# The second weight tile of each in-projection unit split by ScalarE and an accumulating DMA instead of VectorE

## The chip, the core and the metric

The kernel runs on one core of a Trainium2 chip. The metric is the device time of one execution in microseconds, taken as the median of several runs. The engines are TensorE (PE), which multiplies matrices; VectorE (DVE) and ScalarE (ACT), which work on tiles in the on-chip memories; GpSimd (POOL), a slower general engine; and SyncE (SP), which here only issues DMAs. Each engine takes its instructions in one fixed order and waits where the next one's data is not there. A DMA issued by POOL stands in POOL's order like any other instruction.

## What is computed

Two layers of a recurrent decoder run over a prompt of 512 positions and 8 sample sequences of 8, 576 columns in all. The part of a layer that matters here, cut from the reference:

```python
proj = (h @ lw['w_in']).astype(f32)
(hg_q, hg_f, hg_i, hg_g, gla_q, gla_k, gla_v, gla_a, gla_g, rw_cols,
 ret_q, ret_k, ret_v, ret_g, gate_logits) = _split(proj, IN_WIDTHS)
# four recurrent mixers (HGRN2, GLA, RWKV-7, RetNet) on their columns
up = jnp.einsum('blnc,ncd->blnd', branches, lw['w_branch'])
merged = jnp.sum(gates * up, axis=2).astype(h.dtype)
y = merged @ lw['w_out']
# then x + y, and x + SwiGLU(RMSNorm(x))
```

`h` is the normalised input with 1024 features; all weights are float32.

## The kernel before

All large products are made in float16 with both operands split in two: a float32 weight w becomes `hi`, the float16 of WS·w, and `lo`, the float16 of WS·w − hi. For each 128 by 128 block PE runs three matmuls, hi·hi (L241), hi·lo of the input (L242) and lo·hi (L243), in `gemm`. Only L243 reads the weight's `lo`.

The input projection is cut into units of 128 output columns, 46 in each layer. `w_in` calls `wload` for one: 1024 rows are 8 blocks of 128, so a unit has two tiles of 128 by 512, g = 0 with blocks 0 to 3 and g = 1 with blocks 4 to 7 (PE goes through blocks 0 to 3 first). SP loads a tile into one of four `raw` buffers (float32); ACT writes `hi` (L228), DVE writes `lo` (L229), both into a `whl` tile of a ring of four ("w"; the first two units of a layer use a ring "rd"). `wload` is also called for the branch, output and feed-forward weights.

The units of a layer follow a fixed list in `mix_units`: six HGRN units first, then RWKV, GLA, the rest of HGRN, and the RetNet units with the gate columns between and behind them. `mix` advances them in turn with generators that run the recurrences of the units before, so that PE has projection work while DVE and ACT work on the recurrences. The order of instructions on each engine comes out of a scheduler that walks this program; a reader sees it in the order rows further down. In the HGRN stage ACT computes tanh and a scaled copy of a projection (L498 `th`, L499 `pcp`, written as a gated product by DVE in L500), loads function tables, and evacuates `hg_v` (L487); POOL computes `gd` (L980, L981) from `hg_q` and `hg_k`. In the start of a layer ACT squares the input (L306), takes the norm's root (L319, L320), and casts the normalised input to `h` (L464), which PE waits for. In the gate units ACT evacuates the projection (L1458) and the mixed tokens (L248 `bo` and `mt`). POOL's L901 is a large product in the RWKV part, and L1709 an accumulating DMA in the feed-forward part, from one float32 buffer onto another.

Of the kernel before, what the change touches and what calls it, by code (L numbers as in the profile page):

```python
# [13 lines left out]
AF = mybir.ActivationFunctionType  # L14
ALU = mybir.AluOpType
PSUM = bass.MemoryType.PSUM
ADD, SUB, MUL, MAX, MIN = ALU.add, ALU.subtract, ALU.mult, ALU.max, ALU.min
# [8 lines left out]
KT = D // 128  # L26
WS = 256.0
# [147 lines left out]
class Net:  # L175
# [29 lines left out]
        return self.pc[:, c:c + 1]  # L205


    def wload(self, pieces, nk, ncols, rings=("w",)):


        nc = self.nc
        step = GW // ncols
        tiles, parts = [], []
        for g, k0 in enumerate(range(0, nk, step)):
            kn = min(step, nk - k0)
            n = kn * ncols
            raw = self.wp.tile([128, GW], F32, tag="raw", name="raw")
            rv = raw[:, :n].rearrange("p (k c) -> p k c", k=kn)
            for ap, off, w in pieces:
                nc.sync.dma_start(out=rv[:, :, off:off + w],  # L220
                                  in_=ap[128 * k0:128 * (k0 + kn)].rearrange("(k p) c -> p k c", p=128))
            if not parts:
                ring, rings = rings[0], rings[1:] or rings
                c = SIZE[ring] // (4 * GW)
                hl = self.t(ring, [128, c, 2, GW], "whl", F16)
                parts = [hl[:, i] for i in range(c)]
            hl = parts.pop(0)
            nc.scalar.activation(hl[:, 0, :n], raw[:, :n], AF.Copy, scale=WS)  # L228
            nc.vector.scalar_tensor_tensor(hl[:, 1, :n], raw[:, :n], WS, hl[:, 0, :n], op0=MUL, op1=SUB)  # L229
            tiles.append(hl[:, :, :n].rearrange("p a (k c) -> p a k c", k=kn))  # L230
        return lambda k: (tiles[k // step][:, 0, k % step], tiles[k // step][:, 1, k % step])

# [245 lines left out]
            yield  # L478

    def w_in(self, l, pieces, n):  # L480
        return self.wload([(self.io["w_in"][l][:, c:c + w], o, w) for c, o, w in pieces], KT, n, self.rings_in)

    def copy_evac(self, dst, scale):
        nc = self.nc
# [1469 lines left out]
```

## Time and profile before

| | us |
|---|---|
| median of 3 runs | 2200.16 |
| lowest, highest | 2197.33, 2200.17 |
| the profiled execution | 2207.72 |
| its span | 2205.9 |
| PE busy | 2039.1 |
| DVE busy | 1636.6 |
| ACT busy | 1081.3 |
| POOL busy | 682.3 |
| in-projection and mixing, layer 0 and layer 1 | 0 to 510, 1100 to 1600 |

Durations further down are of the profiled execution, which took 7.6 us more than the median. The busy times overlap; the chain of waits, followed back from the last instruction, tells which piece of work ended last at each time. A row of a timeline gives start, duration, engine, line, operation and tiles, and in square brackets the idle time before it with what ended it.

### The profile page before, as it was taken

The numbers are of one execution on the slowest core, as the hardware profiler recorded it, in microseconds if no ns is written. First come the engines' busy times: TensorE is split into PE (matmuls) and PEld (weight loads), VectorE is DVE, ScalarE is ACT, GpSimd is POOL, SyncE is SP. The second block draws the span as 40 slices with busy tenths as digits, with TensorE's granted clock in tenths as the row PEclk, the third lists the DMA queues.
The fourth block names the chain that finished last, engine by engine and source line by source line (L and its number), as shares of the span: only waits on it lengthen the run. The fifth ranks groups of instructions, "written<-read, shape, count | busy, mean of one in ns | idle before, by whom it ended". The sixth has DMA issues, their size and how long they took to land.

```text
span 2205.9 us, 42236 instructions
## 1 busy us (share of the span) xinstructions
PE 2039.1 (92%) x15754; PEld 1612.3 (73%) x15754; DVE 1636.6 (74%) x3409; ACT 1081.3 (49%) x2524; POOL 682.3 (31%) x889
## 2 busy tenths in 40 slices
PE   7989999998888899999999889989998988999998
PEld 5767787786676677777777778768776766777776
DVE  7889667768785899863488986586788779998441
ACT  6554546345444555442466355453645465554332
POOL 2223222146550544320012142213465316443000
PEclk9999999999999999999999999999999999999999
DMA  6312224333435344343421222242343443443331
GB/s 181 84 41 62 58 58 110 77 83 92 116 98 177 80 116 120 87 135 103 122 68 46 58 62 60 73 111 62 87 120 88 131 141 97 111 116 87 121 106 51
DMA packets 373498, 209.59 MB, mean 95 GB/s; under 512 B 59810, under 2 KB 360410, under 8 KB 373292
## 3 DMA queue, kind: packets, MB, share of 16 engines
q1 hardware_dynamic: 365516, 192.73, 31.6%
q0 software_dynamic: 7776, 14.16, 3.6%
q8 instruction: 124, 2.03, 0.4%
q14 instruction: 82, 0.67, 0.1%
HBM read 173.72 MB, written 16.59 MB: 86 GB/s over the span
## 4 chain that ended last, share of the span: by engine, by line
PE 47%; DVE 28%; ACT 8%; issue 7%; DMA 5%; POOL 3%; SPq 1%; DVEq 0%; ACTq 0%; POOLq 0%
PE pb L243 5%; PE pb L242 5%; PE pb L241 5%; PE xb L243 4%; PE xb L242 4%; PE xb L241 4%; DVE hA L1704 4%; DVE hS L1704 3%; DVE sc L1745 2%; DVE fy L1776 2%; DVE whl L229 2%; DVE su L1745 2%; PE fsS L1731 2%; PE fsS L1729 2%; PE fsS L1730 2%
## 5 line engine op out<-in xcount | busy, mean ns | idle before, releaser
L241 PE MATMUL pb<-h,whl 128*128 128x288 f16 (+1 forms) x1504 | 435.8, 290 | 4.4 <-ACT h L464 2.2
L243 PE MATMUL pb<-h,whl 128*128 128x288 f16 (+1 forms) x1504 | 435.5, 290 | 3.2 <-DVE whl L229 3.1
L242 PE MATMUL pb<-h,whl 128*128 128x288 f16 (+1 forms) x1504 | 436.0, 290 | 0.6 <-DVE h L465 0.4
L229 DVE SCALAR_TENSOR_TENSOR whl<-raw,whl 128x512 f16<-128x512 f32 (+1 forms) x352 | 253.8, 730 | 134.3 <-ACT whl L228 132.2
L242 PEld LDWEIGHTS <-whl 128*128 128x128 f16 (+1 forms) x2784 | 275.4, 99 | 88.0 <-issue 13.5
L243 PEld LDWEIGHTS <-whl 128*128 128x128 f16 (+1 forms) x2784 | 275.1, 99 | 88.0 <-issue 12.7
L241 PEld LDWEIGHTS <-whl 128*128 128x128 f16 (+1 forms) x2784 | 277.2, 100 | 76.6 <-issue 3.6
L228 ACT ACTIVATE whl<-raw 128x512 f16<-128x512 f32 (+1 forms) x352 | 213.3, 618 | 168.2 <-PE pb L243 51.9
L243 PE MATMUL xb<-fa,whl 128*128 128x288 f16 x704 | 201.3, 286 | 0.0
L242 PE MATMUL xb<-fa,whl 128*128 128x288 f16 x704 | 201.3, 286 | 0.0
L241 PE MATMUL xb<-fa,whl 128*128 128x288 f16 x704 | 201.3, 286 | 0.0
L1729 PE MATMUL fsA<-h,hA 128*128 128x288 f16 x432 | 124.3, 288 | 14.9 <-DVE gu L1550 10.8
L1729 PE MATMUL fsS<-st,hS 128*128 128x288 f16 x456 | 132.6, 291 | 5.9 <-ACT hS L1703 5.9
L1731 PE MATMUL fsS<-st,hS 128*128 128x288 f16 x456 | 132.4, 290 | 0.4 <-DVE hS L1704 0.3
L1730 PE MATMUL fsS<-st,hS 128*128 128x288 f16 x456 | 132.5, 291 | 0.0
L1731 PE MATMUL fsA<-h,hA 128*128 128x288 f16 x432 | 124.2, 288 | 1.7 <-DVE hA L1704 1.6
L1730 PE MATMUL fsA<-h,hA 128*128 128x288 f16 x432 | 124.3, 288 | 0.0
L1707 POOL TENSOR_TENSOR raw<-raw 128x512 f32<-128x512 f32 x52 | 79.0, 1520 | 134.2 <-DVE hA L1704 129.7
L1729 PEld LDWEIGHTS <-hS 128*128 128x128 f16 x864 | 85.7, 99 | 35.9 <-ACT hS L1703 13.7
L1704 DVE SCALAR_TENSOR_TENSOR hA<-sraw,hA 128x512 f16<-128x512 f32 x110 | 103.1, 945 | 10.6 <-ACT hA L1703 10.6
L1707 POOL TENSOR_TENSOR sraw<-sraw 128x512 f32<-128x512 f32 x60 | 89.7, 1499 | 51.4 <-DVE hA L1704 45.7
L1731 PEld LDWEIGHTS <-hS 128*128 128x128 f16 x864 | 85.7, 99 | 24.8 <-DVE hS L1704 2.6
(486 smaller groups left out, 5257.8 us busy)
## 6 DMA issues: line engine op xcount, KB each, us to landing
raw<-in_w_in SPq DMA_DIRECT2D x208, 256.0 KB
sraw<-in_w_ffn_in SPq DMA_DIRECT2D x40, 512.0 KB
raw<-in_w_ffn_out SPq DMA_DIRECT2D x80, 256.0 KB
raw<-in_w_ffn_in SPq DMA_DIRECT2D x78, 256.0 KB
x<-xd SPq DMA_DIRECT2D x32, 288.0 KB
raw<-sraw POOLq DMA_DIRECT2D x34, 256.0 KB, 3.3
sraw<-in_w_in SPq DMA_DIRECT2D x32, 256.0 KB
raw<-in_w_out SPq DMA_DIRECT2D x32, 256.0 KB
```

The costliest lines, as they stand in the source:

```text
L228: nc.scalar.activation(hl[:, 0, :n], raw[:, :n], AF.Copy, scale=WS)
L229: nc.vector.scalar_tensor_tensor(hl[:, 1, :n], raw[:, :n], WS, hl[:, 0, :n], op0=MUL, op1=SUB)
L241: nc.tensor.matmul(ps, wh, hi, start=i == 0, stop=False)
L242: nc.tensor.matmul(ps, wh, lo, start=False, stop=False)
L243: nc.tensor.matmul(ps, wl, hi, start=False, stop=i == len(ks) - 1)
L1704: nc.vector.scalar_tensor_tensor(hl[:, 1], a, WS, hl[:, 0], op0=MUL, op1=SUB)
L1707: nc.gpsimd.tensor_tensor(dst, a, b, op=op)
L1729: nc.tensor.matmul(ps, w[a][:, 0, k], hi, start=k == 0, stop=False)
L1730: nc.tensor.matmul(ps, w[a][:, 0, k], lo, start=False, stop=False)
L1731: nc.tensor.matmul(ps, w[a][:, 1, k], hi, start=False, stop=k == 3)
L1745: nc.vector.tensor_tensor(o, a, p, op=ADD)
L1776: nc.vector.scalar_tensor_tensor(y, u, PH * AS, sg, op0=MUL, op1=MUL)
```

## The change

`wload` hands the split to a new function, `wsplit`. For in-projection tiles with g = 1, 92 in the kernel, `lo` and `hi` are made without DVE. ACT writes −w as float16 into `lo` (L212). POOL issues a DMA that adds `lo`, cast to float32, onto the raw tile in place, so the raw tile holds w minus its float16 rounding (L213). ACT makes `hi` as −WS·lo (L214), which does not need the DMA, and, when the DMA has landed, writes `lo` as WS times the raw tile (L215). All other tiles keep the old pair, which now has the lines 217 and 218. From there on a line of the kernel after is 11 higher than the same line before (L228 and L229 are the exception: they moved into `wsplit`).

```diff
@@ -205,7 +205,19 @@
         return self.pc[:, c:c + 1]
 
-    def wload(self, pieces, nk, ncols, rings=("w",)):
+    def wsplit(self, hi, lo, w, dma):
+
+        nc = self.nc
+        if dma:
+            nc.scalar.activation(lo, w, AF.Copy, scale=-1.0)
+            nc.gpsimd.dma_start(out=w, in_=lo, accum_op=ADD)
+            nc.scalar.activation(hi, lo, AF.Copy, scale=-WS)
+            nc.scalar.activation(lo, w, AF.Copy, scale=WS)
+        else:
+            nc.scalar.activation(hi, w, AF.Copy, scale=WS)
+            nc.vector.scalar_tensor_tensor(lo, w, WS, hi, op0=MUL, op1=SUB)
+
+    def wload(self, pieces, nk, ncols, rings=("w",), dma=False):
 
         nc = self.nc
@@ -225,8 +237,7 @@
                 hl = self.t(ring, [128, c, 2, GW], "whl", F16)
                 parts = [hl[:, i] for i in range(c)]
             hl = parts.pop(0)
-            nc.scalar.activation(hl[:, 0, :n], raw[:, :n], AF.Copy, scale=WS)
-            nc.vector.scalar_tensor_tensor(hl[:, 1, :n], raw[:, :n], WS, hl[:, 0, :n], op0=MUL, op1=SUB)
+            self.wsplit(hl[:, 0, :n], hl[:, 1, :n], raw[:, :n], dma and g % 2)
             tiles.append(hl[:, :, :n].rearrange("p a (k c) -> p a k c", k=kn))
         return lambda k: (tiles[k // step][:, 0, k % step], tiles[k // step][:, 1, k % step])
 
@@ -478,7 +489,7 @@
             yield
 
     def w_in(self, l, pieces, n):
-        return self.wload([(self.io["w_in"][l][:, c:c + w], o, w) for c, o, w in pieces], KT, n, self.rings_in)
+        return self.wload([(self.io["w_in"][l][:, c:c + w], o, w) for c, o, w in pieces], KT, n, self.rings_in, True)
 
     def copy_evac(self, dst, scale):
         nc = self.nc
```

Names of tiles count up through the program, so the numbers of one tile differ between the two kernels; the sentences say which belong together.

At the start of layer 0, on ACT. Before, between the squares of the first half of the norm and the casts of h:

```order
L228 ACTIVATE whl_150<-raw_148 128x512
L306 ACTIVATE xsq_215,xss_176<-xin_131 96x512
L228 ACTIVATE whl_150<-raw_153 128x512
L319 ACTIVATE xr_171<-xr_171,eps_117 96x3
L320 ACTIVATE xr_171<-xr_171 96x3
L464 CAST h0_139<-nrm_238 128x288
L464 CAST h1_140<-nrm_242 128x288
L464 CAST h2_141<-nrm_246 128x288
```

After; whl_150 is the first unit in both, raw_153 its second tile:

```order
L217 ACTIVATE whl_150<-raw_148 128x512
L317 ACTIVATE xsq_217,xss_178<-xin_131 96x512
L212 ACTIVATE whl_150<-raw_153 128x512
L330 ACTIVATE xr_173<-xr_173,eps_117 96x3
L214 ACTIVATE whl_150<-whl_150 128x512
L331 ACTIVATE xr_173<-xr_173 96x3
L215 ACTIVATE whl_150<-raw_153 128x512
L475 CAST h0_139<-nrm_240 128x288
L475 CAST h1_140<-nrm_244 128x288
L475 CAST h2_141<-nrm_248 128x288
```

The second tile's three ACT instructions now stand around the norm's root (L319 before, L330 after), the last ahead of the first cast.

In the HGRN stage of layer 0, on ACT. Before, whl_735 is the second tile of the unit whose counterpart after is whl_743:

```order
L228 ACTIVATE whl_735<-raw_733 128x512
L1228 ACTIVATE hg_f_302<-hg_f_302,lb_562 128x576 x2
L1229 ACTIVATE hg_k_303<-hg_f_302 128x576 x2
L1239 ACT_TABLE_LOAD
L1239 ACTIVATE hg_l2_682<-hg_l2_682 128x576
L1240 ACTIVATE hg_f_302<-hg_f_302 128x576
L1239 ACTIVATE hg_l2_689<-hg_l2_689 128x576
L1240 ACTIVATE hg_f_302<-hg_f_302 128x576
L498 ACT_TABLE_LOAD
L498 ACTIVATE th_723<-pb_698 128x288
L499 ACTIVATE pcp_724<-pb_698 128x288
```

After, with `hg_v` now at L498:

```order
L509 ACT_TABLE_LOAD
L509 ACTIVATE th_731<-pb_706 128x288
L510 ACTIVATE pcp_732<-pb_706 128x288
L215 ACTIVATE whl_743<-raw_741 128x512
L509 ACTIVATE th_773<-pb_748 128x288
L510 ACTIVATE pcp_774<-pb_748 128x288
L217 ACTIVATE whl_807<-raw_805 128x512
L212 ACTIVATE whl_812<-raw_810 128x512
L498 ACTIVATE hg_v_778<-pb_779 128x288
L214 ACTIVATE whl_812<-whl_812 128x512
```

The L215 of whl_743 stands behind a table load and the first th/pcp pair, where the old kernel had that tile ready ahead of hg_f (L1228). In the rows left out ahead of these, whl_743's L212 and L214 stand where its L228 stood.

In the same stage, on POOL. Before:

```order
L465 TENSOR_TENSOR h5_144<-nrm_405,h5_144 128x288
L980 TENSOR_TENSOR gd0_911<-hg_q_304,hg_k_303 128x4
L981 TENSOR_TENSOR gd0_911<-hg_q_304,hg_k_303 128x8
L980 TENSOR_TENSOR gd0_911<-hg_q_304,hg_k_303 128x4
L981 TENSOR_TENSOR gd0_911<-hg_q_304,hg_k_303 128x8
L574 TENSOR_SCALAR rw_g_896<-cur_897 128x1
```

After, with the DMAs of the new split:

```order
L476 TENSOR_TENSOR h5_144<-nrm_411,h5_144 128x288
L213 DMA raw_679<-whl_681 128x512
L213 DMA raw_741<-whl_743 128x512
L991 TENSOR_TENSOR gd0_925<-hg_q_310,hg_k_309 128x4
L992 TENSOR_TENSOR gd0_925<-hg_q_310,hg_k_309 128x8
L991 TENSOR_TENSOR gd0_925<-hg_q_310,hg_k_309 128x4
L992 TENSOR_TENSOR gd0_925<-hg_q_310,hg_k_309 128x8
L213 DMA raw_810<-whl_812 128x512
L213 DMA raw_876<-whl_879 128x512
L213 DMA raw_951<-whl_953 128x512
L585 TENSOR_SCALAR rw_g_910<-cur_911 128x1
```

The DMAs of whl_681 and whl_743 stand ahead of the four `gd` instructions (L991 and L992, before L980 and L981), and those of the next three tiles behind them.

In a gate unit at the end of the stretch of layer 0, on ACT. Before; whl_6377 is a second tile:

```order
L228 ACTIVATE whl_6377<-raw_6375 128x512
L812 COPY rtk_6421<-tkp_6417 128x384
L864 ACTIVATE rsd_6495<-rsd_6495,reb_4913 128x128
L793 COPY kvb0_580<-rkp_5111 64x64
L794 COPY kvb0_580<-rw_v_2907 64x64
L793 COPY kvb0_580<-rkp_5111 64x64
L794 COPY kvb0_580<-rw_v_2907 64x64
L1458 ACTIVATE gth_6435<-pb_6400 128x288
L248 ACTIVATE bo_6199<-rt_o_5231 128x576
L248 ACTIVATE mt0_6437<-mty_6445 128x288
L248 ACTIVATE mt4_6441<-mty_6447 128x288
```

After; its counterpart is whl_6467:

```order
L212 ACTIVATE whl_6467<-raw_6465 128x512
L823 COPY rtk_6513<-tkp_6509 128x384
L214 ACTIVATE whl_6467<-whl_6467 128x512
L875 ACTIVATE rsd_6587<-rsd_6587,reb_4981 128x128
L259 ACTIVATE bo_6287<-rt_o_5305 128x576
L1469 ACTIVATE gth_6527<-pb_6492 128x288
L259 ACTIVATE mt0_6529<-mty_6537 128x288
L259 ACTIVATE mt4_6533<-mty_6539 128x288
L259 ACTIVATE mt2_6531<-mty_6543 128x288
L215 ACTIVATE whl_6467<-raw_6465 128x512
L259 ACTIVATE mt6_6535<-mty_6541 128x288
```

L214 stands one instruction behind L212, and L215 behind the evacuation of the gate (L1469, before L1458) and three copies of mixed tokens (L259, before L248). PE's order is the same in both but for some places at the start of each layer.

## Rows read from the trace of the kernel before

**Rows 1.** The page: span, busy time by engine, chain by engine, the DVE split.

```profile
span 2205.9 us, 42236 instructions
...
PE 2039.1 (92%) x15754; PEld 1612.3 (73%) x15754; DVE 1636.6 (74%) x3409; ACT 1081.3 (49%) x2524; POOL 682.3 (31%) x889
...
PE 47%; DVE 28%; ACT 8%; issue 7%; DMA 5%; POOL 3%; SPq 1%; DVEq 0%; ACTq 0%; POOLq 0%
...
L229 DVE SCALAR_TENSOR_TENSOR whl<-raw,whl 128x512 f16<-128x512 f32 (+1 forms) x352 | 253.8, 730 | 134.3 <-ACT whl L228 132.2
```

**Rows 2.** Windows of both in-projections: length, busy by engine, PE clock, DMA, GB/s.

```profile
0.00:510.00 510.00, 467.59 (x3507) 372.54 (x3508) 383.42 (x955) 267.81 (x692) 141.27 (x276) 0.98 0.32 83
...
1100.00:1600.00 500.00, 466.03 (x3527) 373.48 (x3525) 378.87 (x916) 260.92 (x672) 135.56 (x252) 0.98 0.28 71
```

**Rows 3.** The same view, 55 us windows: recurrent heads, then gate columns.

```profile
110.00:165.00 55.00, 47.24 (x334) 37.00 (x333) 48.62 (x114) 29.68 (x72) 12.05 (x20) 0.91 0.16 40
...
440.00:495.00 55.00, 54.10 (x432) 44.48 (x431) 34.05 (x76) 26.62 (x64) 22.31 (x30) 1.00 0.32 82
```

**Rows 4.** Chain by line (0:510, 1100:1600); then DVE groups of 110:220, 1210:1320.

```profile
by line: PE pb L243 9.9%; PE pb L242 9.9%; PE pb L241 9.8%; issue 5.4%; PE lvp L1026 3.2%; DVE whl L229 3.2%; DMA raw<-in_w_in 2.2%; DVE qt L1122 1.7%; DVE le L1107 1.7%; PE gop L1056 1.6%; DVE sc L1137 1.5%; DVE hg_f L1227 1.4%; ACT whl L2
...
by line: PE pb L243 10.5%; PE pb L242 10.4%; PE pb L241 10.3%; issue 4.6%; PE lvp L1026 3.3%; DVE whl L229 2.9%; DVE mt L250 1.7%; PE gop L1056 1.6%; DVE le L1107 1.6%; DVE hg_f L1227 1.5%; DVE qt L1122 1.4%; DVE sc L1137 1.3%; PE ub L241 1
...
L229 DVE SCALAR_TENSOR_TENSOR whl<-raw,whl 128x512 f16<-128x512 f32 x18 | 14.9, 828 | 0.8 <-ACT whl L228 0.7
...
L229 DVE SCALAR_TENSOR_TENSOR whl<-raw,whl 128x512 f16<-128x512 f32 x19 | 15.8, 834 | 0.8 <-ACT whl L228 0.7
```

**Rows 5.** The chain piece by piece: start us, us, what; five short windows.

```profile
10.09 0.64 ACT whl L228
...
10.76 0.69 DVE whl L229
...
146.32 3.00 DVE whl L229
...
161.73 0.63 ACT whl L228
...
1491.53 0.60 DVE whl L229
```

**Rows 6.** Timeline of POOL, then of DVE, at 146 us: start, duration, what.

```profile
146.14 2.63 POOL L901 TENSOR_TENSOR rw_w<-rw_ub,cst 128x1152 f32<-128x1152 f32 x1 [7.98 <-DVE rw_ub L737]
...
146.24 3.08 DVE L229 SCALAR_TENSOR_TENSOR whl<-raw,whl 128x512 f16<-128x512 f32 x1
```

**Rows 7.** The accumulating DMA L1709: issue ns min/median/max; issue to landing.

```profile
L1709 POOL DMA_DIRECT2D raw<-sraw x34: 862/881/1040, 515.6 to 2017.8; - x34
...
DMA to landing us min/median/max: 3.2/3.2/4.9
```

**Rows 8.** Timeline of ACT, start of layer 0.

```profile
13.78 1.28 ACT L464 CAST h<-nrm 128x288 f16<-128x288 f32 x3 [2.63 <-DVE nrm L463]
...
21.49 1.66 ACT L228 ACTIVATE whl<-raw 128x512 f16<-128x512 f32 x3
```

**Rows 9.** Timelines of ACT, POOL and PE in the HGRN stage of layer 0.

```profile
53.06 0.41 ACT L499 ACTIVATE pcp<-pb 128x288 f32<-128x288 f32 x1
...
55.91 2.93 POOL L980 TENSOR_TENSOR gd<-hg_q,hg_k 128x4 f32<-128x4 f32 x1 [8.04 <-DVE hg_q L500]
...
58.80 0.35 POOL L981 TENSOR_TENSOR gd<-hg_q,hg_k 128x8 f32<-128x8 f32 x1
...
49.84 0.29 PE L243 MATMUL pb<-h,whl 128*128 128x288 f16 x1
...
57.97 0.29 PE L243 MATMUL pb<-h,whl 128*128 128x288 f16 x1
```

**Rows 10.** Timelines of ACT and PE, the tightest gate tile.

```profile
498.12 0.62 ACT L228 ACTIVATE whl<-raw 128x512 f16<-128x512 f32 x1
...
502.65 0.29 PE L243 MATMUL pb<-h,whl 128*128 128x288 f16 x1
```

## The prediction

> **What bounds the kernel now.** The page is read first. TensorE (PE) is busy for 2039 of 2205.9 us, VectorE (DVE) for 74% of the span, ScalarE (ACT) for 49% and GpSimd (POOL) for 31%; yet the chain that ended last gives PE only 47% and DVE 28% [rows 1]. So PE is the engine with most work, and DVE is what it most often waits for. The change touches in-projection tiles alone, so next come the two stretches where layers 0 and 1 do their in-projections, 0 to 510 and 1100 to 1600 us: PE is busy for 467.6 of 510 and 466.0 of 500 us [rows 2]. That leaves 42.4 + 34.0 = 76 us of idle PE, a ceiling for the gain that no faster weight split can pass. Windows of 55 us tell where the idle time lies. At 110 to 165, where the recurrent heads run, DVE is busy for 48.6 us, PE for 47.2, and PE's granted clock is 0.91; at 440 to 495, where the gate columns run, PE is busy for 54.1 of 55 us and DVE for 34.1 [rows 3]. DVE time given back is worth something in the first kind of stretch and nothing in the second.
>
> How much the weight split itself holds up is read from the chain of the two stretches: the DVE split, L229, has 3.2% of 510 us and 2.9% of 500 us [rows 4], which is 16.3 + 14.5 = 30.8 us for first-half and second-half tiles together. The change takes only the second halves off DVE. Piece by piece, the chain holds L229 of a second-half tile 25 times, 18.8 us in all, from 10.76 to 1491.53 us [rows 5].
>
> **What it removes.** 92 L229 of 0.73 us mean [rows 1] leave DVE: 67 us of busy time, of which the 18.8 us lie on the chain. Not all of that is a gain. Three of the pieces are 3.0 us long [rows 5], and the rows say why: at 146.14 POOL starts L901, 2.63 us, and the L229 beside it takes 3.08 [rows 6] instead of 0.7. The next DVE instruction in the order is a scan with two inputs; as four L229 and a POOL instruction of two inputs also stretch each other in the HGRN stage (L980, below), I take it that 3.0 − 0.7 = 2.3 us is handed on to it each time, 6.9 us in all, and 18.8 − 6.9 = 11.9 us is won; if the wait went with L229, 18.8. By the Trainium skill, "SBUF — State Buffer", section "Who interferes with whom", a DVE instruction with two SBUF inputs and a GpSimd one that reads SBUF exclude each other: by that rule it is handed on, and 11.9 stands. To this come the three places where DVE stood at a second-half L229 that waited for ACT's L228, as at 161.73 [rows 5]: 0.63 us of L228 and 0.38 us until DVE's next work began, 1.0 each, 3.0 in all. Gain: **14.9 us**. Bounds: 0, if at each place the next instruction ends at the same time, and more than this, if all DVE work in the stretches that DVE bounds counts (second rival).
>
> **What it adds, and what hides it.** ACT gets two instructions more for each of 92 tiles, 184 x 0.62 = 114 us, onto 1081 us. In the two stretches it is busy for 267.8 and 260.9 us [rows 2], so an added 57 us each leaves it under two thirds; its cover is its own idle time. POOL gets 92 accumulating DMAs. The only such DMA of the trace is L1709, without a cast: 0.88 us of POOL to issue, and 3.2 us from issue to landing, 4.9 at most [rows 7]. Its 256 KB are as many as the new one writes; the new one reads half as many. I take 0.88 and 3.2, the median of the nearest row. POOL then gets 81 us more, 40 for each layer, beside 141 and 136 us [rows 2], with room. The range of the nearest row is 3.2 to 4.9, and both ends are kept; the reading half of the bytes could put it below 3.2, which no row sizes and which would gain at most the 0.6 us of late tiles below and a part of the early losses. A rule of the Trainium skill speaks against 3.2: by "SBUF — State Buffer", section "SBUF: two separate sides", descriptors of a DMA issued from GpSimd cannot be written while DVE is in a two-port mode, so that the landing would come later; no figure follows from it. What bears on it here is that none of L1709's 34 issues of this form took above 1.04 us [rows 7].
>
> The tile's latency grows. Before: L228 0.63 + L229 0.69, about 1.4 us. After: L212 0.63, 0.1 to the issue, 3.2 to the landing, 0.1, L215 0.63, about 4.7 us. The rest is asked of every second-half tile: does PE come to it later than that? Beyond the first 100 us of each layer the order leaves 4 to 17 us for 71 of 73 tiles. The tightest in the gate stretch has its L228 at 498.12 and its lo part is wanted by PE at 502.65 [rows 10]: 498.12 + 4.7 = 502.8, late by some 0.2, and with the copies that ACT's new order puts ahead of L215, 0.4. One more tile is late by 0.2. Loss in the steady part: **0.6 us**. At a landing of 4.9 six tiles are late, by 6.2 us together; at 6.5, 20 tiles, by 28 us. The raw buffer is held 3 to 4 us longer; its load was issued 15 us and more ahead, so nothing is late for that.
>
> The first units have no such cover. (a) Start of layer 0: the first second-half tile's L228 is at 10.09 [rows 5], so L215 ends at about 10.09 + 4.7 = 14.8. In ACT's new order it stands ahead of all h casts, the first of which began at 13.78 [rows 8]: +1.0 us. After it seven split instructions stand ahead of the second norm's root instead of four, three more at 1.66 / 3 = 0.55 us [rows 8]: +1.7. Loss **2.7 us**. (b) The HGRN stage: L215 of tile 743 stands behind ACT's table load and th/pcp, of which the last ran at 53.06 for 0.41 us [rows 9], so its lo is ready at about 54.0. The same tile's matmuls wanted the lo part at 49.84 [rows 9], and PE's new order puts some 1.9 us of other work ahead: 54.0 − 51.7 = 2.3 us late. Then POOL: the DMA of tile 812 is queued behind L980, which ran from 55.91 for 2.93 us beside four L229, and L981, to 59.15 [rows 9]. With two L229 there instead of four I take half of what L980 has above L981's 0.35 off, 1.3 us, so: issue 57.9, landing 61.1, L215 to 61.8; PE wants it at 57.97 [rows 9] plus the 2.3 already lost, 60.3: +1.5. Behind that L215 on ACT wait hg_v and the level exponentials, which DVE waits for; they have the same 1.5, not more. 3.8 for a layer, and layer 1 has the same order: **7.6 us** for both.
>
> **Sum.** 14.9 gained, 2.7 + 7.6 + 0.6 = 10.9 lost: 4.0 us faster. The profiled execution took 2207.72 us, 7.6 above the median of 2200.16, so the same 4 us are taken off the median: **2196 us**. Its own range is 2190 to 2204: gains between 9 and 18, losses between 8 and 13.
>
> **Rivals.** *DVE's place is taken by the next in line.* On the chain the piece goes, but ACT (now fuller) or POOL ends at the same time; gain 0, early losses stay: 2200 + 10.9 = 2211. For it: ACT has 8% of the chain already [rows 1]. Against it: most of the 25 pieces stand between other DVE pieces, as at 146.32 and 1491.53, so that the next DVE work starts when they go. It is also what "the change does not do what it says" would look like: DVE less busy, nothing ended sooner. Chance 0.14.
>
> *DVE's stages shorten by all that leaves.* In 110 to 220 and 1210 to 1320 us DVE runs 18 and 19 L229, 14.9 and 15.8 us [rows 4]; half of it is second-half, 15.4 us. My sum counts 10.5 of chain there less two hand-overs of 2.3, 5.9. If all 15.4 count, the time is 9.5 lower: 2186. For it: DVE is busy for 88% of 110 to 165 [rows 3], and PE's clock there, 0.91, may be granted at full if PE idles less. Against it: the other 12% say that DVE waits too. Chance 0.22.
>
> *The cast DMA lands late* (the other side). Place: the wait of L215 on ACT, in order, with gate and mix evacuations queued behind it and PE behind these. It decides from a landing of about 5 us. Priced from the late tiles: at 4.9, 5.6 us more than in the sum, with ACT's queue behind them twice that, 14.9 − 10.9 − 11 = 7 slower, 2207; at 6.5, 27 more, 2223 and above. For it: POOL issues in order, and L901 or L980 ahead of an issue costs 2.6 to 2.9 us at once [rows 6, 9]; a cast appears in no row. The Trainium skill's rule on descriptors, above, would be one cause of it. Against it: L1709's landing has its median at its least, 3.2 [rows 7]. Chance 0.22.
>
> **Chances.** Forecast 0.42, of which nearly half ends more than 0.2% (4.4 us, about what a measurement of this kernel can tell from no change) faster and nearly all the rest within it. Faster by over 0.2%: 0.19 + 0.22 = 0.41. Slower: late DMA 0.20, no gain 0.10, and 0.02 of the forecast: 0.32. Within: 0.21 of the forecast, 0.06 from edges of the two slower cases: 0.27. Range: 2182 takes in the second rival with its spread; 2216 takes in 2211 and the milder late landings; out are the landings of 6 us and more, and gains above 18.
>
> **What would show it.** Right: no second-half L229; L213 landing near 3.2 us; the 110 to 220 and 1210 to 1320 us stretches about 3 us shorter each, or a little more; ACT at 54%, POOL at 35%; the first h cast behind L215 at about 15 us, and PE waiting for L215 at 54 and 62 us. Wrong: landings of 5 us and up, PE or ACT waiting for the DMA all through the gate stretch (late landing); or DVE 67 us less busy and the chain's share of ACT up by what DVE's went down (no gain). The weakest terms are the landing, which rests on a DMA without a cast, and the early losses, which rest on the order of ACT and POOL and not on a measured wait.

## The result

The changed kernel takes 2231.61 us (median, 2229.81 to 2234.22) against 2199.39 us: 1.0149 of the time before, with an interval of 1.0131 to 1.0166. It is 32 us slower by the medians (33 by the ratio), where 4 us faster was forecast, and the time lies above the range. Ratios below are given with their 95% interval, each against runs of the kernel before on the same chip; 0.1% is 2.2 us.

The page of the kernel after, with the lines that answer to [rows 1] and two lines of the new split:

```profile
span 2228.0 us, 42514 instructions
...
PE 2052.0 (92%) x15754; PEld 1617.7 (73%) x15754; DVE 1574.0 (71%) x3317; ACT 1178.4 (53%) x2708; POOL 743.8 (33%) x981
...
PE 39%; DVE 25%; ACT 10%; issue 9%; DMA 9%; POOL 5%; SPq 1%; DVEq 0%; ACTq 0%; POOLq 0%
DMA raw<-whl 5%; PE xb L254 4%; PE xb L253 4%; PE xb L252 4%; DVE hA L1715 3%; PE pb L254 3%; PE pb L253 3%; PE pb L252 3%; DVE hS L1715 3%; DVE sc L1756 2%; DVE fy L1787 2%; PE fsS L1742 2%; PE fsS L1741 2%; PE fsS L1740 2%; DVE su L1756 2%
...
L213 POOL DMA_DIRECT2D raw<-whl x92 | 80.4, 874 | 391.6 <-ACT whl L212 254.6
...
L215 ACT ACTIVATE whl<-raw 128x512 f16<-128x512 f32 x92 | 57.9, 630 | 105.3 <-DMA raw<-whl 105.0
```

VectorE (DVE) went from 1636.6 to 1574.0 us busy, ScalarE (ACT) from 49% to 53%, GpSimd (POOL) from 31% to 33%, all about as forecast. The chain tells what did not: a DMA `raw<-whl`, which the kernel before does not have, holds 5% of the chain, and L215 has 105.3 us of idle ACT before it, ended by that DMA. The matmuls are as many as before; PE's busy time rose all the same, by 13 us (2039.1 to 2052.0), at a granted clock of 0.974 on the mean, 0.977 before, while the traced span grew by 22 us.

How long the landing took, and who waited, by the rows of L213 and the waits of ACT and of PE (us in total, times, longest):

```profile
L213 POOL DMA_DIRECT2D raw<-whl x92: 850/874/1002, 12.2 to 1603.3; - x92
...
DMA to landing us min/median/max: 2.9/3.1/5.1
```

```profile
ACT whl L215 <- DMA raw<-whl: 105.0, 65, 5.5
...
PE pb L254 <- ACT whl L215: 10.4, 8, 2.2
```

The landing is 3.1 us in the median, for which 3.2 was taken from [rows 7]. It is not the same everywhere: 27 of the 92 take over 3.5 us, and the first one in the kernel, which holds up the first L215, takes 4.7. They go with what else moves: in the 40 cases where the other queues moved less than 50 KB in the 2.9 us behind the issue the median is 3.0 us, in the 11 with over 400 KB 4.3; no run tried this by itself. PE's matmuls waited for a late lo 8 times, 10.4 us. ACT waited for a landing 65 times, 105 us. So on the whole the DMA was not late; what the prediction did not price is that ACT stands still until it lands.

Matched instruction by instruction on PE, the two traces lie apart by some 11 us at 120 us of the span, 15 at the end of layer 0's in-projection, 11 when layer 1 begins, 20 at 1220 and 24 at 1600: of what the in-projections lose, some two thirds go in the first 120 us of each layer.

### The profile page after: what moved, and what is told of

The parts are those of the page before. It is cut to its first block, busy times and chain, and to the rows that moved or that the text cites. A ratio compares the mean times of both kernels' runs of the same rounds, so it can differ in the third digit from the quotient of the medians.

```text
span 2228.0 us, 42514 instructions
## 1 busy us (share of the span) xinstructions
PE 2052.0 (92%) x15754; PEld 1617.7 (73%) x15754; DVE 1574.0 (71%) x3317; ACT 1178.4 (53%) x2708; POOL 743.8 (33%) x981
## 4 chain that ended last, share of the span: by engine, by line
PE 39%; DVE 25%; ACT 10%; issue 9%; DMA 9%; POOL 5%; SPq 1%; DVEq 0%; ACTq 0%; POOLq 0%
DMA raw<-whl 5%; PE xb L254 4%; PE xb L253 4%; PE xb L252 4%; DVE hA L1715 3%; PE pb L254 3%; PE pb L253 3%; PE pb L252 3%; DVE hS L1715 3%; DVE sc L1756 2%; DVE fy L1787 2%; PE fsS L1742 2%; PE fsS L1741 2%; PE fsS L1740 2%; DVE su L1756 2%
## 5 line engine op out<-in xcount | busy, mean ns | idle before, releaser
L254 PE MATMUL pb<-h,whl 128*128 128x288 f16 (+1 forms) x1504 | 437.7, 292 | 11.6 <-ACT whl L215 10.4
L218 DVE SCALAR_TENSOR_TENSOR whl<-raw,whl 128x512 f16<-128x512 f32 (+1 forms) x260 | 182.3, 710 | 109.3 <-ACT whl L217 108.1
L217 ACT ACTIVATE whl<-raw 128x512 f16<-128x512 f32 (+1 forms) x260 | 156.1, 612 | 115.5 <-DMA raw<-in_w_ffn_out 33.6
L213 POOL DMA_DIRECT2D raw<-whl x92 | 80.4, 874 | 391.6 <-ACT whl L212 254.6
L215 ACT ACTIVATE whl<-raw 128x512 f16<-128x512 f32 x92 | 57.9, 630 | 105.3 <-DMA raw<-whl 105.0
L1715 DVE SCALAR_TENSOR_TENSOR hA<-sraw,hA 128x512 f16<-128x512 f32 x110 | 105.0, 962 | 10.4 <-ACT hA L1714 9.7
L1740 PEld LDWEIGHTS <-hS 128*128 128x128 f16 x864 | 85.5, 99 | 35.3 <-ACT hS L1714 14.0
```

What stands on the lines that cost most here:

```text
L213: nc.gpsimd.dma_start(out=w, in_=lo, accum_op=ADD)
L217: nc.scalar.activation(hi, w, AF.Copy, scale=WS)
L218: nc.vector.scalar_tensor_tensor(lo, w, WS, hi, op0=MUL, op1=SUB)
L254: nc.tensor.matmul(ps, wl, hi, start=False, stop=i == len(ks) - 1)
L1715: nc.vector.scalar_tensor_tensor(hl[:, 1], a, WS, hl[:, 0], op0=MUL, op1=SUB)
L1740: nc.tensor.matmul(ps, w[a][:, 0, k], hi, start=k == 0, stop=False)
```

## The experiments

The theory after the result: taking L229 off DVE is worth something, but ACT's wait in its fixed order for each landing costs more. The rivals: ACT's added work, the DMA's traffic or GpSimd's part of it cost the time; or the relief itself is worth nothing. The first four runs take the change apart.

**No lo at all.** What the relief is worth with nothing in its place.

```diff
-            nc.scalar.activation(lo, w, AF.Copy, scale=-1.0)
-            nc.gpsimd.dma_start(out=w, in_=lo, accum_op=ADD)
-            nc.scalar.activation(hi, lo, AF.Copy, scale=-WS)
-            nc.scalar.activation(lo, w, AF.Copy, scale=WS)
+            nc.scalar.activation(hi, w, AF.Copy, scale=WS)
```

> Left out: the lo part of the 92 second tiles. ScalarE writes their hi part as in the kernel before, VectorE has no split for them, there is no DMA, and TensorE reads the hi part a second time in the place of lo, so that the matmuls are as many as before. This is what taking the 92 splits off VectorE is worth when nothing is put in their place. Theory 'relief is real' (the 14.9 us of the prediction): about 2184 us, 12 to 17 faster than before. Rival 'relief is worth nothing' (the next instruction ends at the same time): 2196 to 2200.

Measured: 0.9977 (0.9967 to 0.9987), 5.0 us faster. The relief is real, and a third of the 14.9 us. Its trace shows where a piece of the chain went without a gain. POOL's large product (L901 before, L909 here) and the DVE instruction behind it:

```profile
148.35 2.62 POOL L909 TENSOR_TENSOR rw_w<-rw_ub,cst 128x1152 f32<-128x1152 f32 x1 [8.78 <-DVE rw_ub L745]
...
151.01 2.09 DVE L911 TENSOR_REDUCE rw_uc<-rw_w 128x144 f32<-128x1152 f32 x1 [2.48 <-POOL rw_w L909]
```

Before, a 3.08 us L229 stood beside the product [rows 6]. Without it DVE is idle for 2.48 us, since its next work, the reduction L911, needs the product. The prediction passed 2.3 of the 3.0 us on to a scan and counted 0.7 as won; nothing was won there: what DVE did in that time was free. The rest of the gain does stand where DVE bounds: matched as above, this trace gains some 3.4 us on the trace before between 120 and 180 us and 2.7 between 1140 and 1320, and no lasting gain elsewhere. In the windows of these stretches (columns as in [rows 2]; the kernel before first, then this run) PE gets through 740 and 720 matmuls in 110 us, where it was 716 and 681:

```profile
110.00:220.00 110.00, 98.58 (x716) 77.25 (x714) 98.43 (x262) 54.60 (x152) 33.08 (x61) 0.95 0.21 52
1210.00:1320.00 110.00, 94.65 (x681) 74.95 (x682) 97.78 (x253) 50.98 (x144) 35.70 (x70) 0.95 0.25 62
```

```profile
110.00:220.00 110.00, 98.35 (x740) 77.68 (x738) 93.19 (x256) 59.01 (x159) 31.45 (x61) 1.00 0.22 55
1210.00:1320.00 110.00, 99.92 (x720) 79.33 (x721) 91.79 (x248) 52.29 (x150) 32.04 (x66) 0.95 0.24 61
```

In the first stretch PE is not busier than before (98.35 us against 98.58); its 24 matmuls more come with a granted clock of 1.00 in place of 0.95. In the second the clock is 0.95 in both, and PE is busy for 5.3 us more.

**ACT's work alone; then with the DMA, but without the wait.**

```diff
             nc.scalar.activation(lo, w, AF.Copy, scale=-1.0)
-            nc.gpsimd.dma_start(out=w, in_=lo, accum_op=ADD)
             nc.scalar.activation(hi, lo, AF.Copy, scale=-WS)
             nc.scalar.activation(lo, w, AF.Copy, scale=WS)
```

> The changed kernel without its accumulating DMAs: ScalarE runs all three instructions of a second tile (L212, L214, L215), L215 on the raw tile as it was loaded, so that lo holds another value than the reference needs. ScalarE's added work alone. Theory 'the ordered wait for the landing costs': about 2 to 4 us above the run without lo, near 2188, since ScalarE is busy for half its time. Rival 'ScalarE's added 114 us cost': most of the 32 us loss is here already, 2215 to 2230.

Measured: 0.9987 (0.9975 to 0.9999), 2.9 us faster. The interval overlaps that of the run before it: by the middle values ACT's 114 us cost 2 us, perhaps nothing by the intervals, and its cover held.

```diff
             nc.scalar.activation(lo, w, AF.Copy, scale=-1.0)
-            nc.gpsimd.dma_start(out=w, in_=lo, accum_op=ADD)
             nc.scalar.activation(hi, lo, AF.Copy, scale=-WS)
-            nc.scalar.activation(lo, w, AF.Copy, scale=WS)
+            nc.gpsimd.dma_start(out=w, in_=hi, accum_op=ADD)
+            nc.scalar.activation(lo, hi, AF.Copy, scale=2.0 ** -11)
```

> All of the changed kernel's instructions, 92 accumulating DMAs too, but L215 takes the hi part as its input instead of the raw tile (the DMA adds hi onto the raw tile), so that it waits for ScalarE alone and lo holds another value. The DMA still keeps the raw buffer until it lands, and stands in GpSimd's order. Theory 'the ordered wait costs': within 5 us of the run with three ScalarE instructions and no DMA, 2188 to 2195. Rival 'the DMA itself costs' (GpSimd's queue, the raw buffers, the traffic): 2215 to 2230, near the changed kernel's 2231.6.

Measured: 1.0018 (1.0004 to 1.0031), 4.0 us slower. As many instructions of each kind are there as in the changed kernel, and 29 us of the 33 are gone. Not the wait alone has changed, though: without it the scheduler puts L215 nearer to L212, 3.5 instructions behind it on ACT on the mean, where the changed kernel has some 6. So the 29 us are the price of the wait and of L215's place together; the run with a short landing further down, which keeps the place, tells the two apart. The DMA without a wait costs 6.8 us against none, where neither theory had put so much.

**Where along the layer.** The new split from the 12th unit on, and in the first 11 units alone:

```diff
+        self.nw = getattr(self, "nw", -1) + 1
+        i = self.nw % 46
-        return self.wload([...], KT, n, self.rings_in, True)
+        return self.wload([...], KT, n, self.rings_in, i >= 11)   # or i < 11
```

> The changed split from the 12th in-projection unit of a layer on (70 of 92 tiles); the first 11 units, which run in the first 110 us of a layer, split as before. In the two profiles the changed kernel lost 11 us up to 110 us of layer 0 and 9 us in the same part of layer 1, and 4 and 5 us in the rest. Theory 'the start of a layer has no cover': the 20 us come back, 2208 to 2213. Rival 'the wait is spread over all units': 70 of 92 parts of the loss remain, 2222 to 2226.

> The changed split in the first 11 in-projection units of a layer alone (22 of 92 tiles); all others split as before. Theory 'the loss adds up by units': the changed kernel lost 32.8 us and the later units alone 12.1, so 18 to 22 us slower than before. Rival 'the units share one cause' (each half loses nearly all): above 25 us. Rival 'the first units lose only with the later ones': below 14 us.

Measured: 1.0057 (1.0042 to 1.0072) for the later units, 12.5 us slower, which is the theory's loss (its times were counted from 2199, and the runs of the kernel before beside it took 2206 in the median); 1.0103 (1.0079 to 1.0127) for the first ones, 22.7 us slower. They add up to 35 us, the whole loss within the intervals. 22 tiles lose 1.0 us each, the other 70 lose 0.18 each, net of what their relief wins.

**Who waits.** The whole change, but TensorE reads hi a second time instead of lo, so that only ACT depends on the landing:

```diff
-        return lambda k: (tiles[k // step][:, 0, k % step], tiles[k // step][:, 1, k % step])
+        return lambda k: (tiles[k // step][:, 0, k % step],
+                          tiles[k // step][:, 0 if dma and k // step % 2 else 1, k % step])
```

> The changed kernel, DMA and ScalarE's wait for it included, but TensorE reads the hi part of a second tile a second time instead of lo, so nothing on TensorE waits for the landing; only ScalarE does, in its order. Theory 'what is queued behind the wait on ScalarE costs': nearly the whole loss stays, 25 to 33 us slower than before. Rival 'TensorE waits for the late lo part itself' (the term by which the prediction priced it): most of it goes, 3 to 12 us slower than before.

Measured: 1.0132 (1.0098 to 1.0165), 29 us slower. The order on GpSimd is that of the changed kernel, on ACT but for a few instructions, and ACT waits for 66 landings, 105.6 us. TensorE's own wait for lo, the term in which the prediction priced the steady part, is not what costs: with it taken away nearly all stays.

**The length of the wait.** A DMA of 4 of 512 columns, first with L215 free of it, then with L215 waiting for it:

```diff
-            nc.gpsimd.dma_start(out=w, in_=hi, accum_op=ADD)
+            nc.gpsimd.dma_start(out=w[:, :4], in_=hi[:, :4], accum_op=ADD)
```

> As the run in which L215 does not wait, but each DMA moves 4 of 512 columns: the same count of issues on GpSimd and the same waits there, little traffic, and L215 free of it (lo holds another value). The free DMA cost about 7 us against no DMA at all. Theory 'GpSimd's order and issue cost it': within 2 us of the free DMA, 2 to 6 us slower than before. Rival 'the traffic and the longer hold of the raw buffer cost it': back to the run without a DMA, 1 to 4 us faster than before.

```diff
-            nc.gpsimd.dma_start(out=w, in_=lo, accum_op=ADD)
+            nc.gpsimd.dma_start(out=w[:, :4], in_=lo[:, :4], accum_op=ADD)
```

> The changed kernel with a DMA of 4 of 512 columns: L215 waits for its landing as before, but the landing should come sooner than 3.1 us, 2 us or so if most of it is not the bytes. The wait on ScalarE then shrinks by what the landing shrinks, for each of the 65 waits. Theory 'the loss follows the length of the wait': the 29 us between the changed kernel and the free DMA fall by more than a third, to 12 to 22 us slower than before. Rival 'any wait there loses the same, by the instruction's place in the order': 28 us and more.

Measured: 1.0013 (1.0001 to 1.0025) free, 2.9 us slower, the same within the intervals as the full DMA without a wait: the traffic costs nothing that can be seen. With the wait: 1.0057 (1.0042 to 1.0071), 12.5 us. The landing and ACT's waits there:

```profile
DMA to landing us min/median/max: 2.0/2.0/4.5
```

```profile
ACT whl L215 <- DMA raw<-whl: 60.3, 45, 4.1
```

This is the test that keeps L215's place: it stands 5.9 instructions behind L212 here, and with the shorter landing 20 of the 33 us are gone. The wait's price above the free DMA is 9.7 us with a landing of 2.0 us and 60 us of waiting, and 29 us with 3.1 us and 105: by the middle values it rises faster than the wait. (The trace is of the fastest of the nine runs, 2209.05 us, where their median is 2216.70.) Even a few columns leave this form of the split slower than before. The Trainium skill ("DMA: Bandwidth & Descriptors", section "Anatomy of one DMA — SWDGE (gpsimd) path") puts a fixed part of some 2.0 us on such a DMA whatever its size; the trace agrees with its median of 2.0 us for 4 columns.

**The relief without the first units.** As the run without lo, from the 12th unit on:

```diff
+        self.nw = getattr(self, "nw", -1) + 1
-        return self.wload([...], KT, n, self.rings_in, True)
+        return self.wload([...], KT, n, self.rings_in, self.nw % 46 >= 11)
```

> As the run without lo, but from the 12th in-projection unit of a layer on (70 of 92 tiles); in the first 11 units all tiles have both parts. The run without lo in all units won 5.0 us, with 2.4 us lost in the first 60 us of its trace. Theory 'the first units' new order takes back what the relief gives there': 6 to 8 us faster than before. Rival 'the relief is spread evenly over the tiles': 70/92 of 5.0, 3 to 4 us faster.

Measured: 0.9987 (0.9978 to 0.9996), 2.9 us faster. The theory that the first units' order takes gain back falls; 70 of 92 tiles bring about 70/92 of the 5 us.

**GpSimd's issue.** What of the free DMA costs 6.8 us? A first try put the 92 issues on a scratch tile:

```diff
-            nc.gpsimd.dma_start(out=w, in_=lo, accum_op=ADD)
+            self.ns += 1
+            nc.gpsimd.dma_start(out=self.scr[1][:, 4 * (self.ns % 8):4 * (self.ns % 8) + 4], in_=self.scr[0][:, :4], accum_op=ADD)
```

> The run with three ScalarE instructions and no DMA on the raw tile, plus 92 accumulating DMAs of 4 columns on a scratch tile, which wait for no work of ScalarE (lo holds another value). GpSimd's issue time alone, without its wait in order for ScalarE. The small DMA that waits for ScalarE cost 5.7 us against no DMA. Theory 'GpSimd's wait for ScalarE, with work queued behind it, costs': 1 to 4 us faster than before, as without a DMA. Rival 'the 81 us of issue cost': 1 to 5 us slower than before.

Measured: 1.0107 (1.0089 to 1.0124), 24 us slower, but the question is not answered: with nothing to wait for, all 92 issues came between 1.3 and 91.3 us, ahead of GpSimd's part of the norm and of `gd`, and the trace is 29 us behind at 120 us and gains after that. The next run reads 4 columns of the raw tile instead, so that each issue comes with its load:

```diff
+            nc.gpsimd.dma_start(out=self.scr[:, 4 * (self.ns % 8):4 * (self.ns % 8) + 4], in_=w[:, :4], accum_op=ADD)
             nc.scalar.activation(lo, w, AF.Copy, scale=-1.0)
-            nc.gpsimd.dma_start(out=w, in_=lo, accum_op=ADD)
```

> Three ScalarE instructions and no DMA on the raw tile (lo holds another value), plus 92 accumulating DMAs of 4 columns from the raw tile to a scratch tile, which wait for the tile's load and for no work of ScalarE. GpSimd's issue time, spread over the program by the loads, with almost no wait for ScalarE. Theory 'GpSimd's wait for ScalarE costs the 6 to 7 us of the free DMA': 1 to 4 us faster than before. Rival 'the 81 us of issue cost it': 1 to 5 us slower.

Measured: 1.0020 (1.0005 to 1.0034), 4.4 us slower, 7.3 above the run without a DMA. No issue waits for ACT's part of the split there, and the cost is that of the free DMA. So the theory falls that GpSimd's wait for ACT is needed for it. But the rival is not shown by that: in GpSimd's order these issues wait for the loads of their tiles instead,

```profile
  DMA raw<-in_w_in: 359.9, 74
```

360 us before 74 of them, where GpSimd stood idle for 255 us for ACT in the run with the free DMA. What the runs show is that 92 DMAs in GpSimd's order cost some 7 us, though GpSimd is busy for a third of the span; how much of it is the issuing, 92 times 0.87 us, and how much the waiting in order stays open.

**The first units in two parts**, units 1 to 6 and 7 to 11:

```diff
-        return self.wload([...], KT, n, self.rings_in, i < 11)
+        return self.wload([...], KT, n, self.rings_in, i < 6)   # or 6 <= i < 11
```

> The changed split in the first six units of a layer alone (HGRN; 12 tiles in all). The 11 first units together lost 22.4 us. Theory 'the start of a layer has no cover' (late lo parts, as the prediction priced with 10.3): 9 to 13 us slower than before. Rival 'the loop of ScalarE, GpSimd and DMA in the RWKV units costs most': 2 to 7 us slower.

> The changed split in units 7 to 11 of a layer alone (RWKV; 10 tiles in all), which the prediction priced at nothing. In the changed kernel the chain runs there from ScalarE's evacuation of the RWKV columns to GpSimd's token shift, to the DMA behind it in GpSimd's order, to L215, behind which the next evacuation waits. Theory 'this loop costs': 8 to 13 us slower than before. Rival 'nothing there is late by itself': within 4 us of before.

Measured: 1.0084 (1.0065 to 1.0103), 18.5 us, and 1.0045 (1.0029 to 1.0060), 9.9 us slower. Both places cost, and the HGRN units more than either theory had put; together they are 28 us, above the 22.7 us of the first 11 units but within the intervals. The chain of the changed kernel shows how. In layer 1's HGRN units (start us, us, what):

```profile
1114.74 4.32 DMA raw<-whl
...
1119.09 0.04 issue
1119.14 0.07 ACT whl L215
1119.21 0.47 issue
1119.67 0.39 ACT hg_f L1232
...
1120.09 1.28 ACT L455
...
1121.38 0.50 ACT rstd L455
```

The DMA of an L215 holds 4.32 us (a slow landing, the median being 3.1), and behind that L215 on ACT stand the evacuation of `hg_f` and L455, the norm of the layer's second half, for which DVE, the h casts and PE then wait. And in the RWKV units of layer 0:

```profile
85.35 3.06 DMA raw<-whl
...
88.97 0.40 ACT cur L498
...
89.46 0.22 POOL rw_k L585
...
91.47 0.68 POOL rsh L581
...
92.45 0.19 POOL rw_k L587
92.64 3.43 DMA raw<-whl
...
96.15 0.63 ACT whl L215
```

The landing releases ACT, whose next work is `cur`, the evacuation of the RWKV columns; GpSimd's token shift waits for that; the next unit's DMA is queued behind the shift on GpSimd; and the next `cur` waits on ACT behind that DMA's L215. One turn of this loop takes 7 us, and each contains a whole landing.

**A later place for L215.** Its instruction is written where the second tile is first used:

```diff
-            nc.scalar.activation(lo, w, AF.Copy, scale=WS)
+            return lambda: nc.scalar.activation(lo, w, AF.Copy, scale=WS)
```

> The changed kernel, with L215 written in the program where the second tile is first used, not behind L214; the order on ScalarE then has it 6.6 instructions behind L212 on the mean, 6.1 in the changed kernel. Theory 'the order hardly moves, so the wait stays': 28 to 34 us slower than before. Rival 'a later place is enough': 15 to 24 us slower.

Measured: 1.0153 (1.0132 to 1.0174), 34 us slower, no better. That the wait could be avoided by a really different order on ACT is not shown by this run.

**Where VectorE bounds.** Units 12 to 20 alone (9 second tiles of each layer), twice, and units 15 to 20:

```diff
-        return self.wload([...], KT, n, self.rings_in, True)
+        return self.wload([...], KT, n, self.rings_in, 11 <= i < 20)   # or 14 <= i < 20
```

> The changed split in units 12 to 20 of a layer alone, 18 tiles of each layer's 46 in second position being 9, which run in the 55 us windows where VectorE is busiest. Theory 'relief and wait are of the same size there': within 3 us of before. Rival 'VectorE bounds there, so the relief prevails': 4 to 7 us faster. Other rival 'the wait prevails there too': 4 us and more slower.

> The changed split in units 12 to 20 of a layer alone, a second time. Theory 'the relief there prevails by a little': 1 to 5 us faster than before. Rival 'it was the spread of the runs': within 1 us of before or slower.

> The changed split in units 15 to 20 of a layer alone (12 tiles in all). Theory 'the relief follows the tiles taken off VectorE while it bounds': two thirds of the gain of the nine units, 1 to 3 us faster than before. Rival 'the first three units lose': more than the nine units win, 4 us and more.

Measured: 0.9988 (0.9980 to 0.9997), then 0.9992 (0.9980 to 1.0005), and 0.9988 (0.9978 to 0.9998) for the six units. By the middle values some 2 us faster than before, near the limit of what these runs can tell, and one interval of the three takes in no change; of the runs that keep both parts of every weight and their DMA, these alone have a middle value ahead of the kernel before. ACT waited there for 9 landings, 6.4 us in all (first of the three).

**The same tiles split by GpSimd**, without a landing:

```diff
-            nc.scalar.activation(lo, w, AF.Copy, scale=-1.0)
-            nc.gpsimd.dma_start(out=w, in_=lo, accum_op=ADD)
-            nc.scalar.activation(hi, lo, AF.Copy, scale=-WS)
-            nc.scalar.activation(lo, w, AF.Copy, scale=WS)
+            nc.scalar.activation(hi, w, AF.Copy, scale=WS)
+            nc.scalar.activation(w, w, AF.Copy, scale=WS)
+            nc.gpsimd.tensor_tensor(lo, w, hi, op=SUB)
```

> The same nine second tiles of each layer with no DMA: ScalarE writes hi, then scales the raw tile in place, and GpSimd takes the difference (one instruction of 128 by 512, some 1.5 us by the like one in the feed-forward part). VectorE is as free of them as with the DMA, and there is no landing to wait for. Theory 'without a landing the relief shows': 2 to 6 us faster than before. Rival 'GpSimd and VectorE hold each other up, as L901 and L229 did': 2 us and more slower.

Measured: 1.0037 (1.0025 to 1.0050), 8 us slower. DVE's group of `qt` products, with two inputs each, fits the rival; before, then here, between 110 and 220 us:

```profile
L1122 DVE TENSOR_TENSOR qt<-hg_q,le 64x128 f32<-64x128 f32 (+1 forms) x34 | 11.1, 326 | 0.3
```

```profile
L1134 DVE TENSOR_TENSOR qt<-hg_q,le 64x128 f32<-64x128 f32 (+1 forms) x34 | 13.7, 404 | 0.3
```

404 ns each instead of 326. The timeline shows one of them held: GpSimd's subtraction, the pair of `qt` beside it, and a pair with no subtraction beside it.

```profile
139.50 1.27 POOL L214 TENSOR_TENSOR whl<-raw,whl 128x512 f16<-128x512 f32 x1 [1.81 <-issue]
```

```profile
139.47 1.45 DVE L1134 TENSOR_TENSOR qt<-hg_q,le 64x128 f32<-64x128 f32 x2
...
157.69 0.58 DVE L1134 TENSOR_TENSOR qt<-hg_q,le 64x128 f32<-64x128 f32 x2
```

The first of the pair starts before the subtraction and takes its usual 0.28 us; the second takes 1.15 us and ends 0.15 us behind the subtraction. By the Trainium skill ("SBUF — State Buffer", section "Who interferes with whom") such an instruction and one of GpSimd that reads this memory exclude each other; the trace agrees in this 1.15 us in place of 0.29. Over the whole kernel VectorE is busy for 1635.7 us, 1636.6 before, and 1621.5 in the first run with the DMA in these units: the 18 splits that left it are all but taken back.

## Why the prediction was wrong, point by point

**The landing** was right in the median: 3.1 us for 3.2, and the cast hardly matters; with 4 columns in place of 512 it is 1.1 us less. At two of the places that cost most it took 4.7 and 4.3. The cover of ACT's added work was right too, and that of the raw buffers is not contradicted (4.0 us slower with everything but the wait, GpSimd's part in it).

**The step that failed is the one on the latency.** It asked of every second-half tile whether PE comes to it later than the lo is ready, found 71 of 73 covered, and put 0.6 us on the steady part. PE was indeed rarely late. But the same 3 us are a wait in ACT's order, and the prediction did not ask what stands behind L215 there. The price was 29 us, by the difference between the run with the free DMA and the changed kernel; in the run in which only ACT waits 25 of them are there. The steady part alone lost 12.5 us, net of its relief, instead of 0.6.

**The rival "the cast DMA lands late"** had this very place, L215 in ACT's order with evacuations behind it, but let it decide only from a landing of 5 us. It decided already at 2.0 us, with 9.7 us. The point was taken from PE's late tiles and doubled, not from ACT's queue.

**The early losses** were seen at the right places and sized too small: 10.3 us for the HGRN units and the start, 18.5 measured. In layer 0 the start lost 5 us for 2.7: the first h cast came at 17.57 us, not at 14.8, since the landing took 4.7 us and L212 began 1.2 us later than the L228 it replaces. The HGRN stage came out there as forecast: PE waits for an L215 twice, 1.8 us each, where 2.3 and 1.5 had been put. Layer 1 was taken to have the order of layer 0, and so the HGRN stage alone, 3.8 us, as its loss; the run shows 9.8. Its order is another: an L215 that waits 3.7 us stands ahead of the root of the second half's norm, where in layer 0 the L215 just ahead of that root waits for nothing. The RWKV units were priced at nothing and cost 9.9: a loop through three queues that no single tile's slack shows.

**The gain** was three times too large: 14.9 against 5.0. In the two stretches that DVE bounds the sum had 5.9 of chain and two of the three places of 1.0, 7.9 together, and the trace of the run without lo gains 3.4 + 2.7 = 6.1; the pieces at the start and in the gate units, 7 us of the sum, gave nothing that lasted. The rival that all of DVE's freed time counts is far off; the rise of PE's clock that spoke for it came in the first of its stretches (1.00 for 0.95 between 110 and 220 us). At L901 the piece was free, as the idle 2.48 us of DVE show.

**POOL's issues** were put down as having room, 40 us for each layer beside 141; with their waits in POOL's order they cost 7 us. An engine busy for a third of the time still is late where the chain runs through it, and [rows 1] did give POOL 3% of the chain.

With the measured terms: 5.0 gained; 2 for ACT's work; 7 for the DMAs in GpSimd's order; 29 for the wait: 33 slower. The terms are differences from one run to the next, so that they must add up to the whole; each has an interval of 2 to 5 us to either side.

## What to carry to other kernels

A DMA put between two instructions of one engine is a wait in that engine's order: before asking when the consumer needs the data, list what is queued behind the waiting instruction and who waits for that, above all where a loop runs through several queues. A piece on the chain is worth no more than the time until the next thing its successor waits for. A test with the wait removed and all work kept tells whether the work or the order costs; where a scheduler lays out the program, compare the orders first, since the instruction that no longer waits may have moved.

## What the runs showed of the hardware

An accumulating DMA of 128 by 512 with a cast from float16 landed in 3.1 us in the median, one without a cast in 3.2 [rows 7], and one of 128 by 4 in 2.0; the issue held GpSimd for 0.87 us in the median in each case, whatever the bytes. Where 92 issues had nothing to wait for, the rows show 4.6 us for one in the median, but one overlaps the next, and 36 of them took 35.8 us together; they landed in 6.6 us.

PE's clock has two levels, 1.2 and 2.4 GHz, of which a window shows the mean. At the same work of layer 0 it is 0.94 of the full clock before and 0.88 after:

```profile
373.00:428.00 55.00, 48.11 (x355) 38.41 (x353) 45.01 (x107) 23.12 (x50) 10.48 (x21) 0.94 0.37 94
```

```profile
385.00:440.00 55.00, 47.27 (x327) 37.28 (x325) 40.60 (x99) 26.57 (x58) 14.06 (x24) 0.88 0.49 120
```

The first row is of the kernel before, the second of the kernel after, which is some 12 us behind there. PE stood idle for about as long in both (6.9 and 7.7 of 55 us), but its 327 matmuls took 145 ns each of its busy time, the 355 before 136. In both the clock falls twice, each time after one long wait of PE: waits of 3.5 and 3.2 us before, 3.7 and 3.7 after, and the time at the lower level is 6.8 us before and 13.6 after. That the longer waits brought the clock down for longer was not tried by itself.
